# Decoder block: MLP parks from the eleventh channel block on, two Strassen differences in one operation, and FoX attention in the order turn, logits, values

## The chip, the core and the metric

The kernel runs on one core of one Trainium2 chip. The metric is the device time of one execution in microseconds. Before the change it is 1638.0 us (median of 1638.08, 1638.0 and 1636.72). A difference is stated against that kernel on the same chip.

## What is computed

One hybrid decoder block on x of 256 tokens x 2048 channels in float32: a combined input projection; gated linear attention (GLA, 4 heads); forgetting softmax attention (FoX, 8 heads of 128, queries in 128-row blocks); both branches projected, gated and merged; an output projection with LayerNorm; an MLP with LayerNorm; and a per-layer embedding (PLE). What the change touches is the second attention and the MLP:

```python
def fox_attention(q, k, v, log_f):
    s = (jnp.einsum('bhqd,bhkd->bhqk', q_i, kh)
         + c_i[..., :, None] - c[..., None, :])
    s = jnp.where(pos_k[None, :] <= pos_q[:, None], s, -jnp.inf)
    pr = jax.nn.softmax(s, axis=-1)
    return jnp.einsum('bhqk,bhkd->bhqd', pr, vh)
...
def causal_dwconv(h, w, b):
    hp = jnp.pad(h, ((0, 0), (CONV_W - 1, 0), (0, 0)))
    y = b
    for j in range(CONV_W):
        y = y + hp[:, j:j + S, :] * w[j]
    return y
```

The MLP is gelu(dwconv(x W_gate)) * (x W_up), times W_down, with 5632 channels, so 44 blocks of 128.

## The kernel before

**Matmuls.** Each float32 operand is split into a high part (hi) and a remainder (lo), and a product is hi x both plus lo x hi. ScalarE makes hi of a weight tile by `copy` (L130), VectorE makes lo by a subtraction (L254, or L228 in Strassen units), TensorE multiplies (L319 hi, 512 columns; L324 lo, 256 columns). Work comes in units: in the MLP a unit is 128 output channels over all 2048 inputs; its two halves (1024 inputs each) are raw{u}_0 and raw{u}_1, and from them hi{u}_h and lo{u}_h are made. `prep` (L241) loads a unit's two halves on SP's queue, 512 KB each, into a ring of five buffers, and makes hi and lo up to three units ahead (`unit`, L262). SP issues all loads in the order written; a load that must wait for its buffer holds up all loads behind it.

**MLP.** Block n takes unit 136 + 2n (gate, into psg{n}) and 137 + 2n (up, into psu{n}); each unit is 16 pairs of hi and lo matmuls on x1T. After psg{n}: `comb` (ScalarE copies half of it, tmp at L130; VectorE adds, gp at L363), GpSimd clears and copies the convolution's edges (L1452, L1456), VectorE makes the three taps (yc, L1458 and twice L1463), ScalarE the GELU (L1464). After psu{n}: up (L363), the product (L1477), and its hi and lo in hC (ScalarE, and VectorE at L1480). For some pairs of blocks sums of products are made and stored (sums L824, hs L1486, sent by GpSimd at L1490). In the first blocks `pull(1)` brings a step of `affine` (z, L1293): the gain and bias of the first LayerNorm on 128x512, on VectorE.

**Parks.** 43 later units (down projection, PLE gate and others) are "parked": `park_gen` (L187) loads the four 128x512 blocks of such a unit into a 1-MB tile td{i} of a pool of 15 (`s8`; SP, L191), some steps later `park` (L182) subtracts them in place into Strassen's differences (four VectorE operations 128x512, L172) and GpSimd's queue writes the tile to DRAM (L185), from where `prep_s` (L198) loads it when its unit is due (L209). The tiles of this pool hold x1T (4) and, as the MLP goes on, hC0 to hC9 as well. td29 to td42 are parked in the MLP: the last lines of its loop pull one step a block from n = 4 on, with the load at an even n and subtractions and write one step later (L1493 to L1495). 26 further Strassen units take their differences from the ring's two separate tiles.

**FoX.** `fox_gen` (L611) is a generator whose steps stand between units on TensorE. A step i calls `values(i - 2)` (po, L655 and L657), `turn(i - 1)` (three transposes pt of the weights lg against the identity, L648) and `logits(i)` (pl, L621); `softmax(i)` follows a step later on ScalarE and VectorE (lg, L641).

**The order of the work** is that of the program's text with priorities on each engine, decided when the program is built; SP's and GpSimd's queues keep their order. So the change's effect on the order is read from the built programs.

Of the kernel before, what the change touches and what calls it, by code (L numbers as in the profile page):

```python
# [14 lines left out]
ALU = mybir.AluOpType  # L15
# [4 lines left out]
P = 128  # L20
# [67 lines left out]
def tile_block(ctx: ExitStack, tc: tile.TileContext, wu, wfv, wpp, xT_in, x_in, pT_in, wlr,  # L88
               chan, gnorm, lng, ident_in, mask_in, cmask_in, out):
    nc = tc.nc  # L90
# [23 lines left out]
    def s8(shape, dt=F32, name=None):  # L114
        return big.tile(shape, dt, tag="S8", name=name)

    def t1(name):
        return sm.tile([P, 256], F32, tag="t1", bufs=6, name=name)

    def t2(name):  # L120
        return sm.tile([P, 512], F32, tag="t2", bufs=6, name=name)

    def mmtile(name):
        return pmm.tile([P, 512], F32, tag="mm", name=name)

    def mxtile(name):
        return pmx.tile([P, 512], F32, tag="mx", name=name)

    def copy(o, i, scale=1.0):
        return nc.scalar.activation(o, i, AF.Copy, bias=0.0, scale=scale)  # L130
# [31 lines left out]
    def lo_tile(u, name):  # L162
        o = place(u)[1]
        return rlo.tile([P, 1088], F32R, tag="lo", name=f"lo{name}")[:, o:o + 1024]

    def hi_tile(u, name):
        o = place(u)[0]
        return rhi.tile([P, 1088], F32R, tag="hi", name=f"hi{name}")[:, o:o + 1024]

    def differences(r0, r1, h, pinned=False):  # L170
        b12, b11, b22, b21 = r0[:, 0:512], r0[:, 512:1024], r1[:, 0:512], r1[:, 512:1024]
        sub = lambda o, a, b: nc.vector.tensor_tensor(o, a, b, ALU.subtract)  # L172
        if h == 0:
            i = sub(b11, b12, b11)
            if pinned:
                tc.keep_in_program_order(i)
            sub(b12, b12, b22)
        else:
            sub(b22, b22, b11)
            sub(b21, b21, b22)  # L180

    def park(w, i):  # L182
        for h in range(2):
# [14 lines left out]
    def prep_s(u):  # L198


        r0, r1 = [ring.tile([P, 1024], F32, tag="raw", bufs=5, name=f"raw{u}_{h}")
                  for h in range(2)]
        b12, b11, b22, b21 = r0[:, 0:512], r0[:, 512:1024], r1[:, 0:512], r1[:, 512:1024]
        rt = (r0, r1)
        if u in parked:
            nc.sync.dma_start(b11, wu[u, :, 512:1024])
            nc.sync.dma_start(r1, wu[u, :, 1024:2048])
            w = s8([P, 2048], name=f"td{u}")
            nc.sync.dma_start(w, td[parked[u]])  # L209
            rt = (w[:, 0:1024], w[:, 1024:2048])  # L210
        else:
            for h, r in enumerate((r0, r1)):
                nc.sync.dma_start(r, wu[u, :, h * 1024:(h + 1) * 1024])
        if dn0 <= u < dn0 + NF:
            nh = (u - dn0) // (NF // 2)
            pair = DN_ORDER[nh][(u - dn0) % (NF // 2)]
            i = DN_S[0].index(pair)
            if i % 2 == 0:
                two = s8([P, 8, 256], F32R, name=f"hS{nh}_{pair}")
                nc.sync.dma_start(two.bitcast(F32), sd[i // 2].rearrange(  # L220
                    "p (i n) -> p i n", i=8))
                hS[nh, pair], hS[nh, DN_S[0][i + 1]] = two[:, 0:4], two[:, 4:8]

        def split(src, name, e=slice(0, 1024)):
            hi = hi_tile(u, f"{u}_{name}")[:, e]
            lo = lo_tile(u, f"{u}_{name}")[:, e]
            copy(hi, src)
            nc.vector.tensor_tensor(lo, src, hi.bitcast(F32), ALU.subtract)  # L228
            return [(hi[:, o:o + 512], lo[:, o:o + 512]) for o in range(0, src.shape[1], 512)]

        x11, = split(b11, "b11", slice(512, 1024))
        x22, x21 = split(r1, "b2")
        if u not in parked:
            differences(r0, r1, 0)
        t3, t1_ = split(rt[0], "t13")
        if u not in parked:
            differences(r0, r1, 1)
        t2_, t4 = split(rt[1], "t24")
        ready[u] = [x11, x21, x22, t1_, t3, t2_, t4]
# [245 lines left out]
    for u in range(8):  # L485
        hi, lo = fvu[u]
        for j in range(2):
            kt = 2 * u + j
            a = xT[kt // 4][:, kt % 4, :]
# [6 lines left out]
            for t, i, c in seq:  # L496
                o, n = fch[c]
# [35 lines left out]
    for t in range(2):  # L533
        for c, (o, n) in enumerate(fch):
            n = min(n, 1024 - o)
# [75 lines left out]
    def fox_gen():  # L611


        lgs, sts, ptss = {}, {}, {}
        halves = ((256, 128), (0, 256))

        def logits(h):
            pl = mxtile(f"pl{h}")
            q, k = [fqk[h // 4][:, h % 4, i] for i in range(2)]
            for t, (o, n) in enumerate(halves):  # L620
                nc.tensor.matmul(pl[:, o:o + n], lhsT=q[:, t * P:t * P + P], rhs=k[:, 0:n],  # L621
                                 start=True, stop=True)
            lg = lgs[h] = t2("lg")[:, 0:384]
            for t, (o, n) in enumerate(halves):
                nc.vector.scalar_tensor_tensor(lg[:, o:o + n], pl[:, o:o + n],
                                               ct[:, t * FH + h:t * FH + h + 1],
                                               ncb[:, h * 256:h * 256 + n], ALU.add, ALU.add)
            nc.vector.tensor_tensor(lg[:, P:384], lg[:, P:384], cmask, ALU.add)
            st = sts[h] = sm.tile([P, 8], F32, tag="fst", name="fst")
            nc.vector.tensor_reduce(st[:, 0:1], lg[:, 256:384], AX.X, ALU.max, negate=True)  # L630
            nc.vector.tensor_reduce(st[:, 1:2], lg[:, 0:256], AX.X, ALU.max, negate=True)

        def softmax(h):
            lg, st = lgs[h], sts.pop(h)
            for t, (o, n) in enumerate(halves):
                nc.scalar.activation(lg[:, o:o + n], lg[:, o:o + n], AF.Exp,
                                     bias=st[:, t:t + 1], scale=1.0,
                                     accum_out=st[:, 2 + t:3 + t])
            nc.vector.reciprocal(st[:, 4:6], st[:, 2:4])
            for t, (o, n) in enumerate(halves):  # L640
                nc.vector.tensor_scalar(lg[:, o:o + n], lg[:, o:o + n], st[:, 4 + t:5 + t],  # L641
                                        None, ALU.mult)

        def turn(h):
            lg = lgs.pop(h)
            pt = mxtile(f"pt{h}")
            for i, d in enumerate((1, 2, 0)):
                nc.tensor.transpose(pt[:, d * P:d * P + P], lg[:, i * P:i * P + P], ident)  # L648
            pts = ptss[h] = t2("pts")[:, 0:384]
            copy(pts, pt[:, 0:384])  # L650

        def values(h):
            pts = ptss.pop(h)
            po = mmtile(f"po{h}")
            nc.tensor.matmul(po[:, 0:256], lhsT=fv[:, 0, h * P:h * P + P], rhs=pts[:, 0:256],  # L655
                             start=True, stop=False)
            nc.tensor.matmul(po[:, 128:256], lhsT=fv[:, 1, h * P:h * P + P],  # L657
                             rhs=pts[:, 256:384], start=False, stop=True)
            dst = ofT[h // 4][:, h % 4, :]
            copy(dst[:, 0:256], po[:, 0:256])  # L660
            nc.vector.tensor_tensor(dst[:, 256:512], po[:, 0:256],
                                    dst[:, 0:256].bitcast(F32), ALU.subtract)

        for i in range(FH + 2):
            for f, h in ((values, i - 2), (turn, i - 1), (logits, i)):
                if 0 <= h < FH:
                    f(h)
            yield
            if i < FH:
                softmax(i)  # L670
            yield
# [4 lines left out]
    parks = [park_gen(stored[:7], 2, 0)]  # L676
    load_consts2()
    mixers.append(fox_gen())
    for n in range(16):
        h, j = n // 2, n % 2  # L680
# [115 lines left out]
    for n in range(16):  # L796
        nm, dst, sc = (("q", gq, 1.0 / 16.0), ("k", gk, 1.0))[n // 2 % 2]
        h, c = n // 4, n % 2
# [355 lines left out]
    for n in range(PSM1, 32):  # L1154
        if n in (26, 28):
            i = n // 2 - 13
# [290 lines left out]
    for n in range(NF):  # L1447
# [18 lines left out]
        u = t1("up")  # L1466
# [4 lines left out]
        if pair in DN_S[0]:  # L1471
            if j == 0:
                yp = t2("yp").rearrange("p (k t) -> p k t", t=S)
            h = yp[:, j, :]
        else:
            h = y
# [4 lines left out]
        if pair in DN_S[0] and j == 1:  # L1481
            v = s_sums(yp)
            for i in range(2):
# [5 lines left out]
                o = k % 2 * 1024 + 512 * i  # L1489
                nc.gpsimd.dma_start(sd[k // 2, :, o:o + 512],  # L1490
                                    w.rearrange("p i n -> p (i n)").bitcast(F32))
        if n >= 4:
            pull(1)  # L1493
        if n >= 4:
            pull(1, parks)  # L1495


# [207 lines left out]
def _sst(w, orders, ssets):  # L1705


    out = []
    for nh, (order, sset) in enumerate(zip(orders, ssets)):
        for n in order:  # L1710
            b = [[w[(2 * n + j) * P:(2 * n + j + 1) * P,
                    nh * 1024 + c * 512:nh * 1024 + c * 512 + 512] for c in range(2)]
                 for j in range(2)]
            out.append(np.concatenate([b[0][1], b[0][0], b[1][1], b[1][0]] if n in sset
                                      else b[0] + b[1], 1))
    return np.stack(out)

# [67 lines left out]
```

## Time and profile before

| | |
|---|---|
| three runs | 1638.08, 1638.0, 1636.72 us |
| the profiled execution | 1637.74 us, its span 1635.9 us, granted clock 1.0 |
| TensorE (PE) busy | 1629.3 us, 100% |
| VectorE (DVE) busy | 1356.9 us, 83% |
| ScalarE (ACT) busy | 909.5 us, 56% |
| GpSimd (POOL) busy | 91.2 us, 6% |
| DMA | 477.81 MB, mean 292 GB/s |
| FoX's inserts | 72 to 193 us of the span |
| the MLP's units | 842 to 1312 us |

The span is what the trace holds; the execution's time is 1.84 us longer. In a row of the timeline stand start, duration, engine, line, operation, output and inputs, and in brackets the idle time ahead of it and what ended it. In a row of the groups stand the count, the busy time and the mean of one in ns. In a row of the windows stand the stretch, its length, and by engine busy time and count. Matmuls overlap, so a matmul's duration of 390 ns is more than its step of about 227 ns.

### The profile page before, as it was taken

The numbers are of one execution on the slowest core, as the hardware profiler recorded it, in microseconds if no ns is written. First come the engines' busy times: TensorE is split into PE (matmuls) and PEld (weight loads), VectorE is DVE, ScalarE is ACT, GpSimd is POOL, SyncE is SP. The second block draws the span as 40 slices with busy tenths as digits, with TensorE's granted clock in tenths as the row PEclk, the third lists the DMA queues.
The fourth block names the chain that finished last, engine by engine and source line by source line (L and its number), as shares of the span: only waits on it lengthen the run. The fifth ranks groups of instructions, "written<-read, shape, count | busy, mean of one in ns | idle before, by whom it ended". The sixth has DMA issues, their size and how long they took to land.

```text
span 1635.9 us, 23491 instructions
## 1 busy us (share of the span) xinstructions
PE 1629.3 (100%) x8422; PEld 1396.6 (85%) x8422; DVE 1356.9 (83%) x1964; ACT 909.5 (56%) x1277; POOL 91.2 (6%) x244
## 2 busy tenths in 40 slices
PE   9999999999999999999999999999999999999998
PEld 9988888888888888888898888888888888888887
DVE  7698899788989867878987888888887788988787
ACT  6655555456666653446574455555455456566554
POOL 0000000000000000000010111110111000000000
PEclk9999999999999999999999999999999999999999
DMA  8799899878888758889856898888776679899574
GB/s 325 283 370 345 292 390 353 293 262 299 308 322 326 253 189 320 304 317 393 299 181 198 321 347 322 292 310 312 282 252 221 204 273 339 307 355 344 166 260 156
DMA packets 114838, 477.81 MB, mean 292 GB/s; under 512 B 13032, under 2 KB 14320, under 8 KB 95136
## 3 DMA queue, kind: packets, MB, share of 16 engines
q1 hardware_dynamic: 105216, 417.57, 71.9%
q0 software_dynamic: 9504, 58.73, 9.0%
q8 instruction: 66, 1.08, 0.3%
q14 instruction: 52, 0.43, 0.1%
HBM read 417.53 MB, written 58.73 MB: 291 GB/s over the span
## 4 chain that ended last, share of the span: by engine, by line
PE 96%; DVE 2%; DMA 1%; ACT 1%; issue 0%; POOL 0%; SPq 0%; ACTq 0%; DVEq 0%; POOLq 0%
PE psm L1006 11%; PE dn L868 10%; PE psu L319 9%; PE psg L319 8%; PE psa L1006 5%; PE psu L324 4%; PE psg L324 4%; PE dn_p L868 4%; PE wo L868 3%; PE gr L868 3%; PE gv L868 3%; PE pg L380 3%; PE psb L1006 3%; PE fv L499 2%; PE gr_p L868 2%; PE gv_p L868 2%
## 5 line engine op out<-in xcount | busy, mean ns | idle before, releaser
L254 DVE TENSOR_TENSOR lo<-raw,hi 128x1024 fp32r<-128x1024 f32 x456 | 551.9, 1222 | 135.7 <-ACT hi L130 134.6
L130 ACT ACTIVATE hi<-raw 128x1024 fp32r<-128x1024 f32 x456 | 476.9, 1057 | 299.0 <-DMA raw<-in_wu_dram 68.4
L319 PE MATMUL psg<-x1T,hi 128*128 128x512 f32 x672 | 231.2, 390 | 0.0
L319 PE MATMUL psu<-x1T,hi 128*128 128x512 f32 x688 | 230.2, 390 | 0.0
L324 PE MATMUL psg<-x1T,lo 128*128 128x256 f32 x672 | 186.2, 277 | 0.6 <-DVE lo L254 0.6
L324 PE MATMUL psu<-x1T,lo 128*128 128x256 f32 x688 | 180.5, 277 | 0.0
L1006 PE MATMUL psm<-hi,xT 128*128 128x512 f32 x512 | 163.1, 393 | 0.0
L319 PEld LDWEIGHTS psu<-x1T,hi 128*128 128x128 f32 x688 | 128.7, 188 | 26.7
L319 PEld LDWEIGHTS psg<-x1T,hi 128*128 128x128 f32 x672 | 126.2, 188 | 26.4
L130 ACT ACTIVATE hi_b<-raw 128x512 fp32r<-128x512 f32 x112 | 93.1, 841 | 68.3 <-DMA raw<-in_wu_dram 16.4
L324 PEld LDWEIGHTS psg<-x1T,lo 128*128 128x128 f32 x672 | 126.1, 188 | 0.9 <-DVE lo L254 0.9
L324 PEld LDWEIGHTS psu<-x1T,lo 128*128 128x128 f32 x688 | 125.3, 188 | 0.6
L172 DVE TENSOR_TENSOR td<-td 128x512 f32<-128x512 f32 x172 | 118.3, 688 | 0.9
L228 DVE TENSOR_TENSOR lo_b<-raw,hi_b 128x512 fp32r<-128x512 f32 x112 | 105.3, 955 | 16.5 <-ACT hi_b L130 16.2
L1006 PEld LDWEIGHTS psm<-hi,xT 128*128 128x128 f32 x512 | 96.2, 188 | 19.6
L228 DVE TENSOR_TENSOR lo_t<-td,hi_t 128x1024 fp32r<-128x1024 f32 x86 | 101.8, 1222 | 12.5 <-ACT hi_t L130 11.7
L130 ACT ACTIVATE hi_t<-td 128x1024 fp32r<-128x1024 f32 x86 | 88.1, 1053 | 31.3 <-DMA td<-td 20.2
L1006 PE MATMUL psm<-lo,xT 128*128 128x512 f32 x256 | 99.9, 390 | 0.0
L868 PE MATMUL dn<-hi,hC 128*128 128x512 f32 x352 | 97.9, 390 | 0.0
L1006 PE MATMUL psa<-hi,oT 128*128 128x512 f32 x256 | 81.3, 392 | 0.0
L868 PEld LDWEIGHTS dn<-hi,hC 128*128 128x128 f32 x352 | 66.0, 188 | 13.6
L1006 PEld LDWEIGHTS psa<-hi,oT 128*128 128x128 f32 x256 | 48.1, 188 | 9.9
(414 smaller groups left out, 3129.4 us busy)
## 6 DMA issues: line engine op xcount, KB each, us to landing
raw<-in_wu_dram SPq DMA_DIRECT2D x525, 512.0 KB, 6.3
td<-in_wu_dram SPq DMA_DIRECT2D x43, 1024.0 KB, 8.7
td<-td POOLq DMA_DIRECT2D x43, 1024.0 KB, 6.7
td<-td SPq DMA_DIRECT2D x43, 1024.0 KB, 8.0
hS<-sd SPq DMA_DIRECT2D x11, 1024.0 KB, 8.9
raw<-in_wu_dram SPq DMA_DIRECT2D x43, 256.0 KB, 7.6
fvraw<-in_wfv_dram SPq DMA_DIRECT2D x13, 524.0 KB, 6.7
sd<-hs POOLq DMA_DIRECT2D x24, 256.0 KB, 5.8
```

Source lines behind the costliest of these rows:

```text
L130: return nc.scalar.activation(o, i, AF.Copy, bias=0.0, scale=scale)
L172: sub = lambda o, a, b: nc.vector.tensor_tensor(o, a, b, ALU.subtract)
L228: nc.vector.tensor_tensor(lo, src, hi.bitcast(F32), ALU.subtract)
L254: i = nc.vector.tensor_tensor(lo, raw, hi.bitcast(F32), ALU.subtract)
L319: nc.tensor.matmul(ps, lhsT=hi[i // 8][:, i % 8 * P:i % 8 * P + P], rhs=act[kts[i] // 4][:, kts[i] % 4, :], start=first and i == 0, stop=l ...
L324: nc.tensor.matmul(ps[:, 256:512], lhsT=lo[i // 8][:, i % 8 * P:i % 8 * P + P], rhs=act[kts[i] // 4][:, kts[i] % 4, 0:256], start=False, s ...
L380: nc.tensor.matmul(bs[j][:, 0:m], lhsT=x, rhs=v[:, o:o + m], start=first and i == 0, stop=last and i == 2)
L499: nc.tensor.matmul(fbk[t][c][:, 0:n], lhsT=x, rhs=w[:, o:o + n], start=kt == 0 and i == 0, stop=kt == 15 and i == 2)
L868: nc.tensor.matmul(ps[:, e], lhsT=x, rhs=w, start=k == 1, stop=k == total.get(id(ps), 3 * ns))
L1006: nc.tensor.matmul(ps[t], lhsT=x, rhs=v, start=first and i == 0 and j == 0, stop=last and i == 3 and j == 2)
```

## The change

Three edits. **One**: the host lays out a Strassen unit's first row as b11, b12 (it was b12, b11), and `differences` makes the first two differences of a parked unit, b12 - b11 and b12 - b22, in one VectorE operation of 128x1024, with b12 broadcast; for the units that aren't parked, whose halves are separate tiles, it keeps two. Loads and splits follow the layout. **Two**: `fox_gen` calls turn, logits, values in place of values, turn, logits. **Three**: the MLP's parks begin at n = 10 in place of n = 4; they end at n = 37 in place of 31.

```diff
     def differences(r0, r1, h, pinned=False):
-        b12, b11, b22, b21 = r0[:, 0:512], r0[:, 512:1024], r1[:, 0:512], r1[:, 512:1024]
-        sub = lambda o, a, b: nc.vector.tensor_tensor(o, a, b, ALU.subtract)
+        b22, b21 = r1[:, 0:512], r1[:, 512:1024]
         if h == 0:
-            i = sub(b11, b12, b11)
-            if pinned:
-                tc.keep_in_program_order(i)
-            sub(b12, b12, b22)
+            two = r0.rearrange("p (i n) -> p i n", i=2)
+            if r0.tensor is r1.tensor:
+                four = bass.AP(tensor=r0.tensor, offset=r0.offset,
+                               ap=[r0.ap[0], [1024, 2], [1, 512]])
+                i = nc.vector.tensor_tensor(two, two[:, 1:2].broadcast_to([P, 2, 512]), four,
+                                            ALU.subtract)
+                if pinned:
+                    tc.keep_in_program_order(i)
+                return
+            nc.vector.tensor_tensor(two[:, 0], two[:, 1], two[:, 0], ALU.subtract)
+            nc.vector.tensor_tensor(two[:, 1], two[:, 1], b22, ALU.subtract)
         else:
-            sub(b22, b22, b11)
-            sub(b21, b21, b22)
+            nc.vector.tensor_tensor(b22, b22, r0[:, 0:512], ALU.subtract)
+            nc.vector.tensor_tensor(b21, b21, b22, ALU.subtract)
...
-            nc.sync.dma_start(b11, wu[u, :, 512:1024])
+            nc.sync.dma_start(b11, wu[u, :, 0:512])
...
-        x11, = split(b11, "b11", slice(512, 1024))
+        x11, = split(b11, "b11", slice(0, 512))
...
-        t3, t1_ = split(rt[0], "t13")
+        t1_, t3 = split(rt[0], "t13")
...
-            for f, h in ((values, i - 2), (turn, i - 1), (logits, i)):
+            for f, h in ((turn, i - 1), (logits, i), (values, i - 2)):
...
-        if n >= 4:
+        if n >= 10:
             pull(1, parks)
...
-            out.append(np.concatenate([b[0][1], b[0][0], b[1][1], b[1][0]] if n in sset
+            out.append(np.concatenate([b[0][0], b[0][1], b[1][1], b[1][0]] if n in sset
```

Most lines of the kernel after stand 6 further down than before (L254 becomes L260, L250 becomes L256); a park's differences stand at L177, L185 and L186, its load at L197, its write at L191.

TensorE at one of FoX's inserts, between two units' matmuls, before:

```order
L324 MATMUL psq_1718<-xT_113,lo_0_1578 128x256
L655 MATMUL po_1735<-pts,fv 128x256
L657 MATMUL po_1735<-pts,fv 128x128
L648 MATMUL pt_1740<-ident,lg 128x128 x3
L621 MATMUL pl_1746<-fqk_1252 128x128
L621 MATMUL pl_1746<-fqk_1252 128x256
L319 MATMUL psq_1718<-xT_114,hi_1_1582 128x512
```

and the same place in the changed kernel:

```order
L330 MATMUL psq_1711<-xT_113,lo_0_1572 128x256
L654 MATMUL pt_1728<-ident,lg 128x128 x3
L627 MATMUL pl_1734<-fqk_1249 128x128
L627 MATMUL pl_1734<-fqk_1249 128x256
L661 MATMUL po_1744<-pts,fv 128x256
L663 MATMUL po_1744<-pts,fv 128x128
L325 MATMUL psq_1711<-xT_114,hi_1_1576 128x512
```

The values' two rows went from the front of the insert to its end; nothing was added or taken away.

VectorE in the MLP from block 8's gp to the lo of unit 156 (block 10's gate), before (td30 is a parked tile, z11 the affine step):

```order
L172 TENSOR_TENSOR td30_8669<-td30_8669 128x512
L363 TENSOR_TENSOR gp8_8844<-psg8_8811,tmp_8846 128x256
L172 TENSOR_TENSOR td30_8669<-td30_8669 128x512
L1458 TENSOR_SCALAR yc_8851<-gp8_8844,chn_116 128x256
L172 TENSOR_TENSOR td30_8669<-td30_8669 128x512
L1463 SCALAR_TENSOR_TENSOR yc_8851<-gp8_8844,chn_116,yc_8851 128x256
L172 TENSOR_TENSOR td30_8669<-td30_8669 128x512
L1463 SCALAR_TENSOR_TENSOR yc_8851<-gp8_8844,chn_116,yc_8851 128x256
L254 TENSOR_TENSOR lo155_1_8866<-raw155_1_8862,hi155_1_8864 128x1024
...
L1463 SCALAR_TENSOR_TENSOR yc_8964<-gp9_8957,chn_116,yc_8964 128x256 x2
L254 TENSOR_TENSOR lo156_0_8916<-raw156_0_8912,hi156_0_8914 128x1024
```

and in the changed kernel:

```order
L1299 TENSOR_TENSOR z11_6943<-z11_6943,lnb01_7490 128x512
L260 TENSOR_TENSOR lo155_1_8823<-raw155_1_8819,hi155_1_8821 128x1024
L369 TENSOR_TENSOR gp8_8801<-psg8_8768,tmp_8803 128x256
L1464 TENSOR_SCALAR yc_8808<-gp8_8801,chn_116 128x256
L1469 SCALAR_TENSOR_TENSOR yc_8808<-gp8_8801,chn_116,yc_8808 128x256 x2
L260 TENSOR_TENSOR lo156_0_8871<-raw156_0_8867,hi156_0_8869 128x1024
```

td30's four subtractions are gone from between the taps; lo155_1 stands ahead of them and lo156_0 behind block 8's taps, where it stood behind block 9's.

SP's queue in the MLP around the load of td42, the last parked tile, before:

```order
L250 DMA raw199_1_11444<-in_wu_dram 128x1024
L191 DMA td42_11491<-in_wu_dram 128x2048
L250 DMA raw200_0_11493<-in_wu_dram 128x1024
L250 DMA raw200_1_11499<-in_wu_dram 128x1024
L250 DMA raw201_0_11550<-in_wu_dram 128x1024
```

and in the changed kernel:

```order
L197 DMA td41_11894<-in_wu_dram 128x2048
L256 DMA raw208_0_11896<-in_wu_dram 128x1024
...
L256 DMA raw211_1_12085<-in_wu_dram 128x1024
L197 DMA td42_12133<-in_wu_dram 128x2048
L256 DMA raw212_0_12135<-in_wu_dram 128x1024
L256 DMA raw212_1_12141<-in_wu_dram 128x1024
```

td42's load went from between units 199 and 200 to between 211 and 212. It reuses the slot of td39 before (three parked tiles earlier), and of td41 after (one earlier), which GpSimd's queue writes out (L191 in the changed kernel) once VectorE has subtracted.

More of the change, by code (lines that the diff above doesn't have):

```diff
@@ L202, in prep_s @@
                   for h in range(2)]
-        b12, b11, b22, b21 = r0[:, 0:512], r0[:, 512:1024], r1[:, 0:512], r1[:, 512:1024]
+        b11 = r0[:, 0:512]
         rt = (r0, r1)
         if u in parked:
-            nc.sync.dma_start(b11, wu[u, :, 512:1024])
+            nc.sync.dma_start(b11, wu[u, :, 0:512])
             nc.sync.dma_start(r1, wu[u, :, 1024:2048])
```

## The prediction

> **What bounds the kernel now.** I read the page of the profile first, then the waits of TensorE, then the chain and the timelines of the places where it waited.
>
> ```profile
> PE 1629.3 (100%) x8422; PEld 1396.6 (85%) x8422; DVE 1356.9 (83%) x1964; ACT 909.5 (56%) x1277; POOL 91.2 (6%) x244
> PEclk9999999999999999999999999999999999999999
> PE 96%; DVE 2%; DMA 1%; ACT 1%; issue 0%; POOL 0%; SPq 0%; ACTq 0%; DVEq 0%; POOLq 0%
> PE warm_ps L140 <- DVE warm L137: 1.2, 1, 1.2
> PE psg L324 <- DVE lo L254: 0.6, 1, 0.6
> ```
>
> The reader is to see that TensorE is busy for 1629.3 of 1635.9 us at full granted clock, that the chain is 96% PE, and that in the whole span it waits for data twice: once at the start, and once, for 0.63 us, inside the MLP. VectorE has 17% of the span free. So an edit on VectorE, SP or POOL is worth something only where it removes that wait or makes another. The profiled execution took 1637.74 us, 0.26 below the median of the three runs (1638.0); sums are made against 1637.74 and 0.26 is added at the end. A measurement of this kernel can tell about 0.2%, 3.3 us, from no change.
>
> Here is the one wait and its cause, from the chain in order of time and TensorE's timeline:
>
> ```profile
> 928.40 0.60 DVE td L172
> ...
> 929.33 0.60 DVE td L172
> ...
> 932.25 1.14 DVE lo L254
> ...
> 935.09 0.60 DVE z L1293
> 935.70 0.35 DVE gp L363
> ...
> 937.17 0.50 DVE yc L1463
> ...
> 937.75 0.42 ACT yc L1464
> 938.17 0.96 ACT hi L130
> ...
> 939.15 1.24 DVE lo L254
> ...
> 940.43 0.39 PE psg L324
> 940.82 0.23 PE psg L319
> ```
> ```profile
> 939.42 0.39 PE L319 MATMUL psg<-x1T,hi 128*128 128x512 f32 x1
> 940.43 0.39 PE L324 MATMUL psg<-x1T,lo 128*128 128x256 f32 x1 [0.63 <-DVE lo L254]
> ```
>
> VectorE was late: td30's subtractions at 928 to 930 and the affine step z stand ahead of psg9's taps, whose GELU stands on ScalarE ahead of hi156_0. TensorE issued its hi matmul at 939.42 and the lo matmul at 940.43. The next hi matmul passes on after 0.23, so 1.01 - 0.23 = 0.8 us is lost here, and the rest of this unit already goes at the slow step shown next, 0.1: I count 0.9. Something more follows it:
>
> ```profile
> 863.23:917.50 54.27, 54.27 (x160) 29.92 (x161) 1.00 0.71 249
> 945.93:1001.27 55.34, 55.34 (x160) 29.94 (x161) 1.00 0.92 338
> 1012.38:1066.65 54.27, 54.27 (x160) 29.92 (x161) 1.00 0.82 301
> ```
>
> These are three stretches, each from just inside one unit's first hi matmul to just before another's, with 160 hi matmuls (ten units) each. The windows leave 0.13 us off at their edges, so ten units take 54.40 us before the wait, 5.44 each, then 55.47 right after it, and 54.40 again from 1012 on, at granted clock 1.00 in all three: 1.07 us more per ten units. The slow stretch holds the ten units to 1001 and ends before 1012; I count eleven, 1.2 us, and call it the slow step of TensorE. With it the wait costs 2.1 us.
>
> **The change part by part.**
>
> *The merged difference.*
>
> ```profile
> L172 DVE TENSOR_TENSOR td<-td 128x512 f32<-128x512 f32 x172 | 118.3, 688 | 0.9
> L254 DVE TENSOR_TENSOR lo<-raw,hi 128x1024 fp32r<-128x1024 f32 x456 | 551.9, 1222 | 135.7 <-ACT hi L130 134.6
> ```
>
> Two subtractions of 688 ns become one of 128x1024. The nearest row of that size is 1222 ns, so a park saves 2 x 688 - 1222 = 154 ns, and 43 parks 6.6 us of VectorE. One that reads an operand twice is not in the trace; I bound it by 1222 and by the 1376 of two. All of it lies beside TensorE, which waits for VectorE once, so it is worth 0. Were that cover gone, it would be worth 0.15 us per park in front of a wait. The new layout of the two blocks loads the same bytes.
>
> *The order in attention.* TensorE's rows at one of the inserts, and the next hi matmul; then ten-odd microseconds behind two inserts:
>
> ```profile
> 98.01 0.55 DVE L641 TENSOR_SCALAR lg<-lg,fst 128x128 f32<-128x128 f32 x2
> ```
> ```profile
> 101.88 0.59 PE L655 MATMUL po<-pts,fv 128*128 128x256 f32 x2
> 102.31 0.39 PE L657 MATMUL po<-pts,fv 128*128 128x128 f32 x2
> 102.53 0.49 PE L648 MATMUL pt<-ident,lg 128*128 128x128 f32 x3
> 102.86 0.82 PE L621 MATMUL pl<-fqk 128*128 128x128 f32 x4
> 103.33 0.58 PE L319 MATMUL psfq<-xT,hi 128*128 128x512 f32 x1
> ```
> ```profile
> 78.78:89.67 10.89, 10.89 (x32) 5.93 (x32) 1.00 0.98 361
> 90.65:101.75 11.10, 11.10 (x32) 5.93 (x32) 1.00 1.01 406
> ```
>
> The same eleven matmuls stay. The values' four start at 101.88 and the turn at 102.53, so the turn moves up by 0.65 us. Its input lg is done at 98.01 + 0.55 = 98.56; 3.3 us of slack remain, and no wait comes. The logits move up by 0.65 too and their results are needed an insert later. So 0 by the waits. But the two stretches of 32 hi matmuls between inserts show both steps again, 10.89 and 11.10 us, in turn. What is last before the hi matmuls is now a value matmul, and I cannot read from the trace which step follows that. With 0.21 us each and some seven such stretches, four of one kind and three of the other, the bounds are -0.6 to +0.8 us. I take 0.
>
> *The parks from n = 10.* In blocks 4 to 9 the td loads, subtractions and stores go away, and blocks 32 to 37 get as many. In blocks 4 to 12 the affine steps then stand alone on VectorE, and lo155_1 to lo156_0 lose the 4 x 688 ns of td30 ahead of them. The wait was 0.63, so it is gone: -0.9, and the slow step behind it, -1.2. What is late next there is nothing that I find: hi156_0 comes at least 1 us earlier.
>
> Behind, td42 (loaded at n = 36) takes the slot of td41 (loaded at n = 34), as the pool is full of hC tiles by then. SP has to wait until td41's write has landed, and it issues all loads in order: raw212_0 and all after it stand behind. The like of td41's subtractions in the trace are those at n = 24, which stand at the same place among the taps:
>
> ```profile
> 1099.45 0.39 PE L319 MATMUL psu<-x1T,hi 128*128 128x512 f32 x1
> ```
> ```profile
> 1100.56 0.36 ACT L130 ACTIVATE tmp<-psg 128x256 f32<-128x256 f32 x1
> ```
> ```profile
> 1100.60 1.42 DVE L172 TENSOR_TENSOR td<-td 128x512 f32<-128x512 f32 x2
> ...
> 1103.19 0.69 DVE L172 TENSOR_TENSOR td<-td 128x512 f32<-128x512 f32 x1
> ```
> ```profile
> 1104.17 0.54 POOL L185 DMA_DIRECT2D td<-td  x1 [1.06 <-DVE td L172]
> ```
> ```profile
> L130 ACT ACTIVATE hi<-raw 128x1024 fp32r<-128x1024 f32 x456 | 476.9, 1057 | 299.0 <-DMA raw<-in_wu_dram 68.4
> ```
>
> Let P be the end of psg's unit, 1099.45 there. The write is issued at 1104.17 = P + 4.72; less 0.15 for the merged operation, P + 4.57. The write lands w later, SP needs some 0.1 us, raw212_0 lands x after that, and hi (1.06) and lo (1.22) are made: P + 4.57 + w + 0.1 + x + 2.28 = P + 6.95 + w + x. TensorE wants lo212_0 three units and one hi issue after P, at 3 x 5.44 + 0.23 = P + 16.55. So the wait is w + x - 9.6. Landing times, shortest, median, longest, from the views of the lines L185 (the write), L191 (a 1-MB load of td) and L250 (a raw load):
>
> ```profile
> DMA to landing us min/median/max: 4.1/6.7/14.9
> DMA to landing us min/median/max: 6.7/8.7/11.7
> DMA to landing us min/median/max: 3.5/6.2/13.8
> ```
>
> raw212_0 is issued 0.4 us behind td42 and shares the engines with it, so x is about a td load's time: 6.7 to 8.7. w is 4.1 to 6.7. The bounds of the wait are 1.2 and 5.8; should raw212_0 pass td42 and land in its own 3.5 to 6.2, the lower end is 0. I take w = 4.6 and x = 7.1, near the shortest, since SP stands still and nothing else is in the queues: 2.1 us. Whether the slow step follows, as after the wait of 939 (eleven units, 1.2 us), is open, since after inserts it comes every other time: 0 to 1.2, and I take 0.6.
>
> [...]
>
> *Where the regular blocks are tight.* From the tap of gp to the end of lo the chain above takes 940.39 - 935.70 = 4.69 us; a unit takes 5.44, and ScalarE's copy of psg stands ahead with 0.36 (its row at n = 24). That leaves 0.3 to 0.4 us of slack at five blocks where the order puts a lo behind the taps (n = 13, 21, 25, 33, 37). I bound it by 0 and 0.5 each and take 0.2 in all.
>
> *Sum*: -0.9 - 1.2 + 2.1 + 0.6 + 0.2 = +0.8; 1637.74 + 0.8 + 0.26 = **1638.8**.
>
> **The rivals.**
>
> *td42's wait is hidden* (w + x under 9.6, a fast write and a raw load that passes td42). For it: raw's 3.5. Against it: no td load under 6.7. Only the old wait goes: 1637.74 - 2.1 + 0.2 + 0.26 = 1636.1.
>
> *SP's wait for td41's write is dear, and the kernel slower.* At the median landings, w + x = 6.7 + 8.7 = 15.4, TensorE waits 5.8 at unit 212 and takes the slow step for 1.2: 1637.74 - 2.1 + 5.8 + 1.2 + 0.2 + 0.26 = 1643.1. With the 0.6 and 0.2 of the sum it outweighs the gain from w + x = 10.9 on; with the whole slow step it is over 0.2% from 13.6. For it: half of all landings are longer than the median. Against: those medians are of full queues.
>
> *TensorE's clock falls in a long wait.* If a wait near the upper bound let the granted clock drop, a unit after it at half clock would cost another 5.4: 1648.5. The one wait on record, 0.63 us, left PEclk at 9, and nothing longer is in the trace. [...]
>
> *The change does nothing there, or attention decides*: were the 939 wait to stay and td42's hidden, 1638.2; with the steps in attention all fast as well as the old wait gone and no new one, 1636.1 - 0.2 - 0.6 = 1635.3, and under 1634.7 only if more slow stretches vanish elsewhere.
>
> **How the numbers follow.** My forecast has 0.50 (its own range 1637.1 to 1640.9), the hidden wait 0.24, the dear wait 0.15, the clock 0.02, the last kind 0.09, about half of it on the fast side. Faster than 1634.7: 0.06, the fast end of the last kind and of the hidden wait. Slower than 1641.3: most of the dear wait, the clock and the upper end of mine, 0.18. Within: 0.76. The range 1635.4 to 1642.2 leaves out a tenth at each end.
>
> **What would show it.** Right: no wait at psg10's lo; one wait of TensorE at psg38 (unit 212) for lo L260 or hi, behind a raw landing, with SP standing before td42's load until td41's write lands. Ten units after 939 take 54.27. pt and pl stand 0.65 earlier, with no wait. The merged operation takes 1222 ns. Wrong: a wait of TensorE elsewhere in the MLP (a tight block), a wait in attention, or none at all.

## The result and the profile after

The changed kernel takes 1642.4 us (median of 8 runs, 1639.98 to 1644.31) against 1637.18 of the kernel before beside it (8 runs, 1636.25 to 1638.93): ratio 1.0029, 95% interval 1.0018 to 1.0040. It is slower by about 5 us, 0.29%, where I had put it within 0.2%; the interval begins at 0.18%. The profiled execution took 1643.58 us, 5.84 more than that of before, with a span of 1641.8.

From the page and the waits of TensorE, after:

```profile
PE 1632.5 (99%) x8422; PEld 1398.1 (85%) x8422; DVE 1351.1 (82%) x1921; ACT 911.8 (56%) x1277; POOL 95.2 (6%) x244
PE psg L325 <- ACT hi L130: 2.2, 1, 2.2
PE warm_ps L140 <- DVE warm L137: 1.2, 1, 1.2
PE fv L505 <- ACT fvhi L130: 0.5, 1, 0.5
PE psg L330 <- DVE lo L260: 0.5, 1, 0.5
```

VectorE has 5.8 us less to do, near the 6.6 that the sum of the merged operation had, and TensorE as many matmuls as before. The wait of 0.63 us at block 10's gate is gone. In its place stand one of 2.2 us for a hi and one of 0.5 for a lo. (The one at fv stands at 12 us, at the start of attention; of two executions of one kernel, td42_later and later_both below, one lists such a wait and the other doesn't.) TensorE's timeline says where the two stand:

```profile
1247.25 0.79 PE L325 MATMUL psg<-x1T,hi 128*128 128x512 f32 x1 [2.22 <-ACT hi L130]
1248.51 0.58 PE L330 MATMUL psg<-x1T,lo 128*128 128x256 f32 x1 [0.47 <-DVE lo L260]
1248.89 0.63 PE L325 MATMUL psg<-x1T,hi 128*128 128x512 f32 x1
1249.32 0.42 PE L330 MATMUL psg<-x1T,lo 128*128 128x256 f32 x1
```

This is psg38, unit 212, where td42's load was put. And the hi matmuls behind the wait take 0.63 us where 0.39 is usual, and a lo follows its hi 0.43 later (1248.89 to 1249.32) where 0.23 is usual. The windows give the reason: behind stretch, length and TensorE's busy time (and in the second row the weight loads') stands the granted clock.

```profile
1247.00:1253.90 6.90, 6.18 (x18) 0.51 0.92 330
1256.46:1311.80 55.34, 55.34 (x160) 29.90 (x161) 1.00 0.78 263
```

The granted clock is 0.50 in each window from 1248 to 1253, so in the first stretch TensorE had half its clock for 6.9 x 2 x (1 - 0.51) = 6.8 us. Two shorter windows show that the fall lies inside the wait:

```profile
1246.70:1247.00 0.30, 0.00 (x0) 1.00 1.03 396
1247.00:1247.30 0.30, 0.05 (x1) 0.58 1.04 423
```

At a mean of 0.58 the last 0.3 x 2 x (1 - 0.58) = 0.25 us of the second are at half, so the clock fell at about 1247.05; the wait began at 1245.03 (1247.25 - 2.22), so the clock fell 2.0 us into it, before the second wait. Behind the stretch, at full clock, come ten units at the slow step, 55.34 us in the same cut that takes 54.27 elsewhere.

To see what each costs, I read the first matmul of the same unit in both timelines, before and then after:

```profile
923.01 0.39 PE L319 MATMUL psu<-x1T,hi 128*128 128x512 f32 x1
1006.88 0.39 PE L319 MATMUL psg<-x1T,hi 128*128 128x512 f32 x1
1251.96 0.39 PE L319 MATMUL psu<-x1T,hi 128*128 128x512 f32 x1
1311.89 0.40 PE L868 MATMUL dn<-hi,hC 128*128 128x512 f32 x1
```
```profile
923.45 0.39 PE L325 MATMUL psu<-x1T,hi 128*128 128x512 f32 x1
1005.23 0.39 PE L325 MATMUL psg<-x1T,hi 128*128 128x512 f32 x1
1256.40 0.39 PE L325 MATMUL psu<-x1T,hi 128*128 128x512 f32 x1
1317.41 0.40 PE L874 MATMUL dn<-hi,hC 128*128 128x512 f32 x1
```

| up to | after less before | change there | what it is |
|---|---|---|---|
| unit 153 | +0.44 | +0.44 | start, attention, output projection |
| unit 168 | -1.65 | -2.09 | block 10's wait and its slow step gone |
| unit 213 | +4.44 | +6.09 | unit 212: wait and half clock |
| the first matmul of the down projection | +5.52 | +1.08 | slow step to unit 223 |
| end of the span | +5.9 | +0.4 | last phases |

Within the 6.09: the two matmuls of unit 212 that waited cost 2.22 + 0.47 by the brackets, 3.4 against an undisturbed start (hi 2.4 late, lo another 1.0), and 2.7 is the half clock behind them (some 5.3 us at half).

The chain of the changed kernel shows what the wait hung on:

```profile
1238.82 0.31 SPq L197
...
1239.22 6.90 DMA raw<-in_wu_dram
...
1246.14 1.07 ACT hi L130
...
1247.23 1.23 DVE lo L260
...
1248.51 0.58 PE psg L330
```

SP issues td42's load (L197) at 1238.8 and raw212_0 right behind it; the half lands 6.9 us later, hi and lo are made, and TensorE goes on. What SP had waited for stands in GpSimd's and VectorE's timelines, and in the landing of the write:

```profile
1231.26 1.22 DVE L177 TENSOR_TENSOR td<-td 128x1024 f32<-128x1024 f32 x1
...
1233.65 0.68 DVE L186 TENSOR_TENSOR td<-td 128x512 f32<-128x512 f32 x1
```
```profile
1234.63 0.54 POOL L191 DMA_DIRECT2D td<-td  x1 [0.25 <-DVE td L186]
```
```profile
td<-td POOLq DMA_DIRECT2D x1, 1024.0 KB, 4.1
```

td41's last subtraction ends at 1234.3, the write is issued at 1234.63 and lands 4.1 us later, at 1238.7, and 0.1 us after that SP moves.

### The profile page after: what moved, and what is told of

Same layout as the page of the kernel before. It is cut to its first block, busy times and chain, and to the rows that moved or that the text cites. A ratio compares the mean times of both kernels' runs of the same rounds, so it can differ in the third digit from the quotient of the medians.

```text
span 1641.8 us, 23449 instructions
## 1 busy us (share of the span) xinstructions
PE 1632.5 (99%) x8422; PEld 1398.1 (85%) x8422; DVE 1351.1 (82%) x1921; ACT 911.8 (56%) x1277; POOL 95.2 (6%) x244
## 3 DMA queue, kind: packets, MB, share of 16 engines
q8 instruction: 66, 1.08, 0.3%
## 4 chain that ended last, share of the span: by engine, by line
PE 96%; DMA 2%; DVE 1%; ACT 1%; issue 0%; SPq 0%; POOL 0%; ACTq 0%; DVEq 0%; POOLq 0%
PE psm L1012 11%; PE dn L874 10%; PE psu L325 9%; PE psg L325 9%; PE psa L1012 5%; PE psu L330 5%; PE psg L330 5%; PE dn_p L874 4%; PE gv L874 3%; PE gr L874 3%; PE pg L386 3%; PE wo L874 3%; PE psb L1012 3%; PE fv L505 2%; PE gr_p L874 2%; PE gv_p L874 2%
## 5 line engine op out<-in xcount | busy, mean ns | idle before, releaser
L260 DVE TENSOR_TENSOR lo<-raw,hi 128x1024 fp32r<-128x1024 f32 x456 | 551.8, 1220 | 144.1 <-ACT hi L130 141.4
L1012 PEld LDWEIGHTS psm<-lo,xT 128*128 128x128 f32 x256 | 48.1, 188 | 9.5
```

The lines of the kernel that those rows point to most:

```text
L260: i = nc.vector.tensor_tensor(lo, raw, hi.bitcast(F32), ALU.subtract)
L1012: nc.tensor.matmul(ps[t], lhsT=x, rhs=v, start=first and i == 0 and j == 0, stop=last and i == 3 and j == 2)
```

## The experiments

Theory A: what td42's load waits for, td41's write, makes the loss, with half clock and slow step behind the wait. Against it stand B (the order in attention or the merged operation makes part of the loss) and, in its own words at each run, that the late blocks or the traffic are worse for themselves. Theory C came from the first eight runs: the late parks gain something, and the merged operation gives part of it back in the output projection.

All were timed against the kernel before on the same chip. The ratio is to its runs, with the 95% interval. The changed kernel has 8 runs, td41_write_late and after_turn214 have 5, the others 11. td42_later and later_both are one kernel on two chips, and so are parks10_td42_later and later_plain.

| kernel | median us | before us | ratio |
|---|---|---|---|
| changed kernel | 1642.4 | 1637.18 | 1.0029 (1.0018 to 1.0040) |
| parks10_alone | 1640.38 | 1636.9 | 1.0020 (1.0011 to 1.0029) |
| fox_alone | 1637.56 | 1636.9 | 1.0001 (0.9992 to 1.0010) |
| merged_alone | 1638.23 | 1636.9 | 1.0007 (0.9998 to 1.0016) |
| td42_later | 1637.24 | 1636.9 | 1.0003 (0.9994 to 1.0011) |
| parks10_td42_later | 1635.81 | 1637.82 | 0.9991 (0.9983 to 1.0000) |
| td42_half_later | 1639.08 | 1637.82 | 1.0013 (1.0004 to 1.0022) |
| td41_write_late | 1647.67 | 1637.82 | 1.0057 (1.0044 to 1.0070) |
| after_turn214 | 1641.76 | 1637.82 | 1.0035 (1.0021 to 1.0049) |
| later_plain | 1636.11 | 1637.49 | 0.9994 (0.9985 to 1.0003) |
| later_fox | 1636.07 | 1637.49 | 0.9993 (0.9984 to 1.0002) |
| later_merged | 1637.2 | 1637.49 | 0.9998 (0.9989 to 1.0007) |
| later_both | 1637.62 | 1637.49 | 1.0002 (0.9993 to 1.0011) |

### The three parts, each alone

The first is the kernel before with one line changed:

```diff
-        if n >= 4:
+        if n >= 10:
             pull(1, parks)
```

> The kernel before with its parks begun at n = 10, nothing else changed. Theory A (td42's load behind td41's write makes all the loss): the wait at block 10's gate is gone, TensorE waits about 3 us or a little more at unit 212, goes at half its clock for some us behind it, and at the slow step from there to unit 223; 4 to 6 us slower than before, as the whole change. Theory B (the order in attention or the merged operation makes part of it): clearly less than the whole change, 0 to 3 us slower.

It came out at 1.0020, 3.5 us slower: most of the loss is here, though the time falls between the two theories (A had 4 to 6 us, B 0 to 3). Its waits in the MLP:

```profile
PE psg L319 <- ACT hi L130: 1.6, 1, 1.6
...
PE psg L324 <- DVE lo L254: 0.8, 1, 0.8
```

The wait at unit 212 is there, 2.4 us in all, and block 10's is gone, but in the profiled execution neither half clock nor slow step followed (granted clock 1.00 from 1239 to 1300, 249 matmuls in the last 42 us of it, where the changed kernel has 244), which is why it took only 1639.75.

The second:

```diff
-            for f, h in ((values, i - 2), (turn, i - 1), (logits, i)):
+            for f, h in ((turn, i - 1), (logits, i), (values, i - 2)):
```

> The kernel before with attention's order turn, logits, values, nothing else changed. Theory A: no wait in attention, within 0.5 us of before; the stretches between inserts change their length by up to 0.3 us each, in all about +0.3. Theory B: 2 us or more slower.

1.0001: nothing to be seen, and no wait at attention's inserts (one of 0.2 us at fv stands at 11 us, before them). One thing was unforeseen. Block 10's wait is not there, in a kernel whose MLP is that of before, but the slow step is. From the windows, ten units from 945 on and ten from 1006 on:

```profile
945.15:1000.49 55.34, 55.34 (x160) 29.91 (x161) 1.00 0.91 340
1006.16:1060.43 54.27, 54.27 (x160) 29.91 (x161) 1.00 0.84 310
```

So the wait of 0.63 us need not be in every execution, and the slow step needs no wait that the profile records.

The third is the first hunk of the diff with the layout, alone.

> The kernel before with the merged difference and the layout alone. Theory A: the one operation takes 1220 ns, VectorE is busy about 6 us less, and the time is within 1 us of before; the wait of 0.63 us at block 10's gate may shrink by 0.15. Theory B (VectorE's time counts): 2 us or more faster.

1.0007, 1.3 us slower at an interval that just holds 1; theory A had it within 1 us. The operation has the length that was expected:

```profile
L177 DVE TENSOR_TENSOR td<-td 128x1024 f32<-128x1024 f32 x43 | 52.3, 1217 | 0.0
```

and block 10's wait stays at 0.6. A wait of 0.4 us at `wo_p` in the output projection is new; the last group is about it.

### td42's load, moved

```diff
-        if n >= 10:
+        if n >= 10 and n != 36:
             pull(1, parks)
```

on the changed kernel: block 36 pulls nothing, so td42 is loaded one block later, behind raw213_1.

> The changed kernel with td42's load and subtraction one block later, so that its load stands behind raw213_1 when td41 has long been written. Theory A: no wait at unit 212, full clock, no slow stretch at 1247 to 1317; about 2 us faster than before (1635) and 7 us faster than the changed kernel. Rival (parks in the late blocks load VectorE, whatever the slot): a wait remains somewhere in blocks 36 to 40, and no more than half of the 7 us comes back.

The loss is gone: 1.0003 against 1.0029, 4.3 us by the ratios, and the profile lists no wait of TensorE but that of the start. The rival falls. Half of theory A's forecast failed, though: it isn't 2 us faster than before. A slow stretch stands in its trace too, in units 204 to 209 (5.55 us each), with no wait listed. The profile also shows that SP still waits:

```profile
1238.72 0.33 SPq L197 DMA_DIRECT2D td<-in_wu_dram  x1
1239.15 3.39 SPq L256 DMA_DIRECT2D raw<-in_wu_dram  x5
```

td42's load goes out at 1238.72, as in the changed kernel, and five raw loads in a heap behind it. But these are loads for units 214 on, which TensorE wants 10.9 us (two units) later. The wait was not removed but put where nobody stands behind it.

The same line on the kernel before, without the other two parts:

> The kernel before with parks from n = 10 and td42's load one block later; order in attention and the two subtractions as before. Theory A (only td42's slot costs anything): no wait at unit 212 and none at block 10's gate; 3 us or more faster than the parks alone (1640.4), and 0 to 2 us faster than before, according to how many executions of before have the wait at block 10. Rival (the late blocks are worse for themselves): 1639 or more.

0.9991: 2 us faster than before by the medians, at an interval that ends at 1.0000, and, by the ratios, 4.7 faster than parks10_alone. It has none of the waits, and no slow stretch in the MLP.

In the next, td42's load stands between the two halves of unit 212 (`prep` pulls it ahead of raw212_1):

```diff
         for h in range(2):
+            if u == 212 and h == 1:
+                pull(1, parks)
             raw = ring.tile([P, 1024], F32, tag="raw", bufs=5, name=f"raw{u}_{h}")
```

> The changed kernel with td42's load between the two halves of unit 212, so that only the second half and what follows stands behind td41's write; TensorE wants that half 2.7 us later. Theory A: a wait of 0 to 1.2 us in the middle of unit 212 in place of 3.2, at full clock; 1636.5 to 1639.5. Rival (the load of 1 MB at this place costs by its traffic, not by the order): near the changed kernel's 1642.

1.0013, between the two, as theory A has it. In the profiled execution SP issued td42's load at 1237.88, 0.9 us earlier than in the changed kernel, and no wait is listed at unit 212, though the slow step runs from there to unit 223 (245 matmuls in the 42 us from 1258, at granted clock 1.00, where parks10_alone has 249); the spread of the runs (1637.53 to 1643.06) suggests that others had one.

Then the write, held back:

```diff
+        if i == 41:
+            nc.gpsimd.tensor_copy(w, w)
         nc.gpsimd.dma_start(td[i], w)
```

> The changed kernel with one copy of td41 on itself on GpSimd (128x2048) ahead of its write, which holds the write back by some 2 us. Theory A: the write lands by so much later and all of it is added to the wait at unit 212, 5 us or more, the clock is at half behind it in every execution, and the time 1645 to 1648. Rival (the wait at 212 comes from elsewhere, the write is not what SP waits for): 1642 to 1643, as the changed kernel.

```profile
1234.94 3.17 POOL L192 COPY td<-td 128x2048 f32<-128x2048 f32 x1
1238.41 0.54 POOL L193 DMA_DIRECT2D td<-td  x1 [0.30 <-POOL td L192]
```
```profile
PE psg L327 <- ACT hi L130: 7.0, 1, 7.0
...
PE psg L332 <- DVE lo L262: 0.5, 1, 0.5
```

The copy took 3.2 us and the write left 3.8 later than in the changed kernel (1238.41 against 1234.63). The wait for hi grew by 4.8 (7.0 against 2.2), and the time by 4.6 by the ratios. All of the delay and some more went through to TensorE (the write itself took 5.7 us to land in place of 4.1, the raw load 6.3 in place of 6.9, and 3.8 + 1.6 - 0.6 is 4.8): SP does wait for this write, and nothing lies in between.

The last of this group adds unit 214 to the units that end in a row of lo and a row of hi matmuls (`TURN`):

```diff
-TURN = range(139, 224, 14)
+TURN = (139, 153, 167, 181, 195, 209, 214, 223)
```

> The changed kernel with unit 214 among the units that end in a row of lo and a row of hi matmuls (L334 to L346), as 209 and 223 do. Theory (such a unit ends the slow step): the wait at 212 stays, the slow stretch ends at unit 214 in place of 223, some 0.9 us less in executions that have it, so 1641.5. Rival (the stretch ends by itself after some 65 us): no change, slow units to 223.

It decided nothing: the wait was there (1.7 and 0.8), but unit 213 already ran at the usual step, so there was no stretch to end. The other traces speak for the theory: each slow stretch in the MLP ends in a unit of `TURN`, at 167 in the kernel before, in fox_alone and in merged_alone, at 181 in after_turn214, td41_write_late and later_both, at 195 in td41_write_late and at 209 in td42_later. That it lasts to 223 in the changed kernel says nothing, since 223 is the MLP's last unit.

These kernels give four waits at the same place, and the granted clock around each. Windows of 1246 to 1260, in the order parks10_alone, after_turn214, the changed kernel, td41_write_late:

```profile
1246.00:1260.00 14.00, 12.16 (x69) 1.00 0.94 310
```
```profile
1246.00:1260.00 14.00, 12.00 (x59) 0.88 0.91 325
```
```profile
1246.00:1260.00 14.00, 12.28 (x53) 0.76 0.92 292
```
```profile
1246.00:1260.00 14.00, 7.56 (x29) 0.63 0.95 353
```

A stretch at the 0.50 that the windows show lowers the mean by half its share, so 14 us x 2 x (1 - mean) gives 0, 3.4, 6.7 and 10.4 us at half. The waits were 1.6 + 0.8, 1.7 + 0.8, 2.2 + 0.5 and 7.0 + 0.5 us. Not all of a stretch is loss: in td41_write_late the clock fell at 1247.2, 2.1 us into the wait, and 4.8 us of the stretch passed before the wait for hi ended. The two longer lengths are about twice and three times the 3.4. The clock fell 2.0 and 2.1 us into the two longer waits, in after_turn214 only behind its 1.7 + 0.8 us in two pieces (1.00 in 1248 to 1249, 0.56 in 1249 to 1251), and behind 1.6 + 0.8 it did not fall. What decides that is not shown by these four.

### What the merged operation costs

The four combinations of the two small parts, all with parks from n = 10 and td42 one block later.

> Parks from n = 10 with td42 one block later, order in attention and two subtractions as before (the kernel parks10_td42_later once more, beside the next three on one chip). Theory C (the late parks gain, the merged operation gives back part): 1 to 2 us faster than before. Rival (what the first look showed was scatter): within 0.5 us of before.

> The same with attention's order turn, logits, values. Theory C: 0 to 0.5 us behind later_plain, from the stretches between inserts; no wait at the output projection at 762 us. Rival (the order in attention gives back the gain): 1.5 us or more behind later_plain.

> The same as later_plain with the merged operation, order in attention as before. Theory C: the write of the parked tile at 743 us is issued about 0.7 us earlier against the td load beside it, that load lands up to 1 us later, TensorE waits 0.4 to 1.0 us at wo_p; 0.4 to 1.3 us behind later_plain. Rival: no wait there and the time of later_plain.

> The whole change with td42 one block later (the kernel td42_later once more). Theory C: 0.5 to 1.8 us behind later_plain, the sum of the two, and still about 5 us ahead of the changed kernel. Rival: as later_plain.

Medians of 11 runs each: 1636.11, 1636.07, 1637.2, 1637.62. Against before, later_plain gains 1.4 us by the medians, as theory C had it, but its interval holds 1. The order in attention costs -0.04 us without the merged operation and 0.4 with it, which I can't tell from the scatter of the runs. The merged operation costs 1.1 without the new order and 1.55 with it; all runs of later_both but one are longer than every run of later_fox. The place is visible: of the eight profiled executions with the merged operation four list a wait of TensorE at wo_p near 762 us, 0.2 to 0.5, and of the six without it none does. The chain of merged_alone runs through it:

```profile
742.89 12.51 DMA td<-td
...
755.80 0.04 ACT hi_t L130
...
762.20 0.61 DVE lo_b L234
...
762.86 0.74 PE wo_p L874 x2
```

The chain comes from a load of a parked tile, issued at 742.89, which lands 12.5 us later. Beside it runs the write of another parked tile on GpSimd's queue. The write's issue in the kernel before, then in merged_alone:

```profile
744.43 0.53 POOL L185 DMA_DIRECT2D td<-td  x1 [19.37 <-DVE td L172]
```
```profile
743.38 0.53 POOL L191 DMA_DIRECT2D td<-td  x1 [20.52 <-DVE td L186]
```

and the load in the kernel before, from its timeline and from the DMA view of 743.15 to 743.7:

```profile
743.21 0.42 SPq L209 DMA_DIRECT2D td<-td  x1
```
```profile
td<-td SPq DMA_DIRECT2D x1, 1024.0 KB, 11.2
```

Before, the write starts 1.22 us behind the load, with the merged operation 0.49, since its subtractions end sooner (VectorE's order changed there too). The load takes 12.5 us in place of 11.2, ScalarE's hi_t comes later, and the wait is at the far end of that chain. The other traces agree: in all six with two subtractions the write is issued 1.2 us behind the load, which lands in 11.2 to 11.9 us; in all eight with the merged operation 0.5 behind, and the load lands in 11.9 to 12.9. That the write's earlier start lengthens the load is argued from these times, not isolated.

The listed waits are less than what is lost there. The first matmul of the output projection and the first behind it, in later_plain, then in later_merged:

```profile
743.81 0.48 PE L868 MATMUL wo_p<-hi_b,mS 128*128 128x512 f32 x1
...
818.96 0.33 PE L1250 MATMUL ptl<-ident,z 128*128 128x128 f32 x1
```
```profile
743.53 0.48 PE L874 MATMUL wo_p<-hi_b,mS 128*128 128x512 f32 x1
...
819.55 0.33 PE L1256 MATMUL ptl<-ident,z 128*128 128x128 f32 x1
```

The stretch takes 75.15 us, with the merged operation 76.02, and the difference of 0.87 is about that of the two profiled spans (1634.2 and 1635.0). What of the 1.1 to 1.55 in the medians lies elsewhere stays open.

## Why the prediction was right and wrong

I had 1638.8 and no change to be told (0.76), with a range that ends 0.2 us below the 1642.4 that was measured. As a difference it is further off: I had +0.8, at most +4.2 (1642.2 - 1638.0), and 5.2 came out against the runs of before beside it. The mechanism was there, as the rival that ends slower; the sizes were not.

**The bound** held: TensorE sets the time, and all of the result but the 0.4 us at each end of the table was found in the waits, the clock and the steps of TensorE.

**The merged operation, taken at 0**, was mis-sized. The time on VectorE came near what was worked out (1217 ns for 1222; 5.8 us less busy for 6.6). But I asked only whether its time was on the path, not what its earlier end sets off. It costs 1.1 to 1.55 us by the medians of the last group.

**The order in attention, at 0 within -0.6 to +0.8**: right (1.0001; -0.04 and 0.4 in the last group).

**The wait at block 10, -0.9 - 1.2**: right against the profiled execution (-2.09 to unit 168), but that execution was one with the wait. fox_alone shows the same MLP without it. Of the four medians of before in the table three lie below the profiled execution, by 0.25 to 0.84 us, and one 0.08 above, where I had added 0.26. The gain that is left in the medians is the 1.1 us (ratio 0.9993) or so of later_plain and later_fox, at the edge of what can be told.

**td42's wait, 2.1 + 0.6**: the mechanism was right in place, cause and order, and its size was the step that failed. Unit 209 starts at 1228.46:

```profile
1228.46 0.39 PE L325 MATMUL psu<-x1T,hi 128*128 128x512 f32 x1
```

That is P. The landings were near what I took: w 4.1 (4.6), x 7.3 (7.1). The write's issue was not: P + 6.17 in place of P + 4.57. Block 24 of before was a poor stand-in, since there VectorE began td's subtractions at P + 1.15 and here at P + 2.80: hs stands right ahead of them in both places, and here it began at P + 2.13 in place of P + 0.48. With the 1.6 more, 0.5 less and 0.2 more, 2.1 becomes 3.4, which is what TensorE lost.

**The clock in a long wait** had 0.02, since I tied it to a wait near 5.8 us. It came 2.0 us into a wait of 2.7 in all and cost another 2.7. With the slow step at its full 1.1 in place of 0.6, the place costs 7.2 us in the profiled execution where I had 2.7. In the medians the slot costs 4.3 (changed kernel against td42_later) to 4.7 (parks10_alone against parks10_td42_later), since not every execution has the half clock and the slow step.

**The tight blocks, 0.2**: no wait showed there.

**The rivals**: "SP's wait is dear" won. That its time came near (1643.1 against 1642.4) is chance, since the reason was another: not landings at the median, but a later start and the clock. Its 0.15 and the clock's 0.02 were too little.

## What to carry to other kernels

Ask of each buffer that a moved transfer reuses how many uses back its last reader is: at distance one, in a queue that issues in order, the wait falls on everything that is queued behind (here td42's load left 0.1 us after td41's write had landed, and raw212_0 right behind it, whose hi TensorE then waited 2.2 us for), and moving that one load to where the next two units' data are already on their way gave back 4 to 5 us. Take a wait's price from the place itself and not from a like one twelve blocks earlier, and look at the granted clock wherever the matrix engine waits some 2 us or more: at three of four such waits here, of 2.4 to 7.5 us, it fell to half. An engine that finishes earlier also starts its transfers earlier, so look at what they then run beside (here a write issued 0.49 us behind a load in place of 1.22, and that load landing in 12.5 us in place of 11.2).

## What the hardware showed that I had not expected

The matrix engine's granted clock fell to half, 0.50 in the windows, at three waits of 2.5 to 7.5 us in all, for 3.4, 6.7 and 10.4 us, and stayed at 1.00 at one of 2.4. At the two longer ones it fell 2.0 and 2.1 us after the last matmul, inside the wait.

At granted clock 1.00 TensorE ran the MLP's pairs of a 512- and a 256-column matmul at two steps, 54.40 or 55.47 us for ten units. Each slow stretch in the MLP of these traces lasted to a unit in which the order of the matmuls changes (three of them to 223, where the MLP ends). Four of them follow a wait (in before, merged_alone, the changed kernel and td41_write_late), none follows the waits of parks10_alone and after_turn214, and in fox_alone, td42_later and td42_half_later one began without any recorded wait. What starts it is open.
